# Two-layer decoder step: gate and value products on half the depth, seven for eight; down in parts of four; low parts of plain weights by adding transfers

## The chip, the cores and the metric

The kernel runs on one core of a Trainium2 chip. A core has five engines with instruction streams of their own: PE (TensorE, matrix products into PSUM), DVE (VectorE), ACT (ScalarE), POOL (GpSimd) and SP (SyncE, which here issues most transfers); 16 DMA engines move data between HBM and SBUF. The metric is device microseconds of one execution. It is taken over several runs, and the profile is of one further execution by the hardware profiler.

## The reference

One inference step of a decoder with two layers. Layer 0 mixes tokens by sliding-window attention, layer 1 by gated linear attention; each is followed by a feed-forward with a causal convolution of width 3 on its gate. There are 512 new rows of one sequence (the prompt) and 8 single rows (the samples). The model is 1024 wide, the feed-forward 2816. All is fp32. What the change touches is the feed-forward and the normalisation around it:

```python
def conv_ffn(x, buf, w_up, conv_w, conv_b, w_down):
    h = x @ w_up                                   # 1024 -> 2 * 2816
    a, u = h[..., :D_FF], h[..., D_FF:]            # gate, value
    ap = jnp.concatenate([buf.astype(a.dtype), a], axis=1)
    c = conv_b + sum(conv_w[j] * ap[:, j:j + T] for j in range(CONV_W))
    y = (jax.nn.gelu(c, approximate=False) * u) @ w_down
    return y, ap[:, T:]

# in each layer i, after the mixer:
xp = layer_norm(ALPHA * xp + mp, ln_mix_g[i], ln_mix_b[i])
fp, cp = conv_ffn(xp, buf0, ffn_w_up[i], ffn_conv_w[i], ffn_conv_b[i], ffn_w_down[i])
xp = layer_norm(ALPHA * xp + fp, ln_ffn_g[i], ln_ffn_b[i])
```

## The kernel before

Activations lie transposed: 128 features on the partitions, rows of tokens along the free axis. The 520 rows are two groups: a has 256 prompt rows, b has 256 prompt rows and the 8 samples (264). A matrix product of fp32 is made of three products in a shorter format (fp32r): each operand is split into a high part (a rounded copy, by ACT) and a low part (what is left, by DVE), and high x high, high x low and low x high are summed in PSUM.

All weights are loaded in *units* of 128 output features: one tile of 128 x 1024 (8 depth steps of 128). `plan` lists the units in order; `phases` marks where stretches of them begin. For layer 0: q, k, v and attention, then eight units of the output projection, then the feed-forward. For layer 1 the same with the gated linear attention. In the feed-forward, the 22 blocks of 128 gate and value features come in three parts, `FF_PARTS` = (0..6, 6..14, 14..22): for each block a unit for the gate and one for the value, and after each part eight down units of that part's depth, which add into x. The last part's down units also carry the normalisation (`ln_chunk`, `ln_end`).

`order` sets the order of the work: each unit is done for a and for b, a leading by four or five units. `load_unit` (L152) loads a unit: a transfer by SP into a `raw` tile (two buffers), then ACT makes `wh` (L167) and DVE `wl` (L170) in one of six weight slots; in the feed-forward there is a seventh slot, `wx`. `run` loads the next unit as soon as b's use of one is done. For a few units behind the start of a stretch the two conversions are issued later (`parts`, L181 and L183), so that they don't stand before the normalisation.

`product` (L186 to L205) issues the three matmuls of each depth step, with 256 or 264 columns. `product2` (L208 to L222), which group a uses in blocks 4 to 21 and in down parts 0 and 1, has high and low part of a's rows side by side and makes the two products with the high weights by one matmul of 512 columns; its two halves are added afterwards by DVE (L641, L663, L686). `ffn_gate` evacuates the gate from PSUM, applies the three taps and Gelu; `ffn_value` multiplies by the value and splits the result into `hh` and `hl` for down. PSUM has eight banks: four `accp` accumulators here, four for the rest (`mps`: two `sc`, one `tp`, one `pv`).

The scheduler that builds the engines' streams orders instructions by a planned timeline where no dependence or written order forbids it; on PE matmuls of neighbouring units can thus stand between one another.

After the normalisation that follows the mixer, POOL adds the bias to x (`ln_end`, L361) late, one chunk per unit, since only down needs it.

Of the kernel before, what the change touches and what calls it, by code (L numbers as in the profile page):

```python
# [11 lines left out]
F32 = mybir.dt.float32  # L12
F32R = mybir.dt.float32r
# [17 lines left out]
FF_PARTS = ((0, 6), (6, 14), (14, 22))  # L31
# [15 lines left out]
EXTRA = 1  # L47
XEND = 8
ACCS = 4

# [10 lines left out]

WIDE = 4
# [35 lines left out]
class Net:  # L98
    def __init__(self, tc, ctx, I, O):
# [9 lines left out]
        self.acc = pool("acc", ACCS, space=PSUM)  # L109
        self.mps = pool("mps", space=PSUM)  # L110
        self.dram = pool("dram", 2, space=DRAM)
# [38 lines left out]


    def load_unit(self, u, pieces=1, extra=False, late=False):  # L152
# [4 lines left out]
        r = self.raw.tile([P, KD * P], F32, name="raw")  # L157
        pool = self.wx if extra else self.wts
        h, l = (pool.tile([P, KD * P], F32R, name=name) for name in ("wh", "wl"))
        n = nt * P // pieces  # L160
        for c in (slice(i * n, (i + 1) * n) for i in range(pieces)):
# [8 lines left out]
            nc.vector.tensor_tensor(l[:, c], r[:, c], h[:, c].bitcast(F32), op=ALU.subtract)  # L170
        self.w[u] = (h, l)

# [35 lines left out]
    def product2(self, g, u, rs, rh, rl, wide):  # L208


        if rs is None or not wide:
            return self.product(g, u, rh, rl), None
        nc = self.nc
        h, l = self.w[u]
        nt = self.units[u][1]
        ps = self.acc.tile([P, 512], F32, name="accp")
        o = ps.rearrange("p (j t) -> p j t", t=2)
        for k in range(nt):
            ks = slice(k * P, (k + 1) * P)
            last = k == nt - 1  # L220
            both = lambda: nc.tensor.matmul(o, h[:, ks], in_turn(rs[:, k].rearrange("p t q j -> p t (q j)")), start=k == 0, stop=last)  # L221
            low = lambda: nc.tensor.matmul(o[:, :P], l[:, ks], in_turn(rh[:, k]), start=False, stop=False)  # L222
            for f in (low, both) if last else (both, low):
                f()
        return ps[:, :256], ps[:, 256:]
# [59 lines left out]
    def ln_end(self, g, i, last=False):  # L285
# [71 lines left out]
        if g.i == 0:  # L357
            self.norm = self.slot + HOLD, self.exp, v.ins, xl.ins, self.next_phase() + 1
        for m in range(KD):
            yield 1 if m else LATEB  # L360
            self.tc.keep_in_program_order(nc.gpsimd.tensor_scalar(x[:, m], x[:, m], 1.0, bi(m), op0=ALU.mult, op1=ALU.add))  # L361
# [243 lines left out]
    def ffn_open(self, layer):  # L605
        nc = self.nc
        if EXTRA:
            self.wx, self.wx_cm = self.open(f"wts{layer}", EXTRA)
# [564 lines left out]
```

## Time and profile before

| | |
|---|---|
| time, median of 2 runs | 1134.0 us (1132.05 to 1135.95) |
| span of the profiled execution | 1131.7 us |
| mean granted clock of PE | 0.991 |
| HBM read, written | 108.67 MB, 8.47 MB |
| share of the DMA engines, queue of SP | 32.8% |

The span runs from the first to the last instruction of the profiled execution; what lies around it belongs to the time of a run and not to the span. The page of the profile gives each engine's busy time, 40 slices of the span, the queues, the chain of work that ended last, and the costliest groups of instructions; other views give the same for a stretch or in order of time. In a row of a timeline stand start, length (both us), engine, line of the kernel, operation, what it writes and reads, shape and count; in brackets the idle time before it and what ended it. Matmuls are pipelined, so their records overlap, and the distance between two starts tells what one costs. The slices of the two engines with most to do, and what the transfers moved:

```profile
PE   8999999999999999999999999999999999999996
...
DVE  7897579655665566568867778779756665566565
...
GB/s 244 150 178 96 16 75 101 105 103 121 94 105 102 93 100 106 75 134 94 57 90 145 122 178 160 139 111 94 113 98 127 94 98 109 93 96 110 76 64 76
```

The feed-forward of layer 0 runs from about 167 to 530 us, that of layer 1 from about 765 to the end.

### The profile page before, as it was taken

How to read it: one execution, taken by the hardware profiler on the slowest of the kernel's cores; microseconds unless marked ns; L12 is line 12 of the kernel's file. 1: busy time of each engine (PE TensorE's matmuls, PEld its weight loads, DVE VectorE, ACT ScalarE, POOL GpSimd, SP SyncE). 2: the span in 40 equal slices, each digit the busy share in tenths (PEclk: the TensorE clock that was granted, in tenths of full speed). 3: DMA queues.
4: the chain of work that ended last, by engine and by line, in shares of the span. 5: the costliest groups of instructions: out<-in, count | busy, mean ns of one | idle time of the engine just before them, and what ended most of it. 6: DMA issues, size and time to landing. Idle time of an engine off the chain costs nothing.

```text
span 1131.7 us, 22912 instructions
## 1 busy us (share of the span) xinstructions
PE 1104.2 (98%) x8806; PEld 1055.1 (93%) x8806; DVE 777.2 (69%) x1626; ACT 565.7 (50%) x1251; POOL 319.3 (28%) x591
## 2 busy tenths in 40 slices
PE   8999999999999999999999999999999999999996
PEld 7997799999999999999899999899999999999995
DVE  7897579655665566568867778779756665566565
ACT  5677556534553245435455556456524553245433
POOL 4575574400110011255211100374400110001243
PEclk9999999999999999999899999999999999999998
DMA  7553023333233233242124354432333223223222
GB/s 244 150 178 96 16 75 101 105 103 121 94 105 102 93 100 106 75 134 94 57 90 145 122 178 160 139 111 94 113 98 127 94 98 109 93 96 110 76 64 76
DMA packets 53804, 122.81 MB, mean 109 GB/s; under 512 B 6808, under 2 KB 27328, under 8 KB 53696
## 3 DMA queue, kind: packets, MB, share of 16 engines
q1 hardware_dynamic: 51536, 119.47, 32.8%
q10 hardware_dynamic: 2160, 1.89, 0.5%
q8 instruction: 69, 1.13, 0.4%
q14 instruction: 39, 0.32, 0.1%
HBM read 108.67 MB, written 8.47 MB: 104 GB/s over the span
## 4 chain that ended last, share of the span: by engine, by line
PE 77%; DVE 10%; DMA 5%; ACT 3%; issue 2%; POOL 1%; SPq 0%; ACTq 0%; DVEq 0%; POOLq 0%
PE accp L198 16%; PE accp L200 16%; PE accp L202 16%; PE accp L221 15%; PE accp L222 8%; DMA vb<-dv 2%; DVE xs_a L355 1%; DVE wl L183 1%; DVE wl L170 1%; DMA raw<-in_w_up 1%; DMA qs<-hl 1%; DVE sgla L910 1%; DVE x_a L353 1%; PE pv L554 1%; ACT pr L523 1%
## 5 line engine op out<-in xcount | busy, mean ns | idle before, releaser
L170 DVE TENSOR_TENSOR wl<-raw,wh 128x1024 fp32r<-128x1024 f32 (+2 forms) x172 | 207.0, 1205 | 103.3 <-ACT wh L167 102.7
L198 PE MATMUL accp<-xh_b,wh 128*128 128x264 f32 x976 | 272.5, 279 | 1.8 <-ACT xh_b L354 1.7
L167 ACT ACTIVATE wh<-raw 128x1024 fp32r<-128x1024 f32 (+2 forms) x168 | 173.6, 1033 | 199.8 <-PE accp L200 187.3
L202 PE MATMUL accp<-xh_b,wl 128*128 128x264 f32 x976 | 270.8, 277 | 0.0
L200 PE MATMUL accp<-xl_b,wh 128*128 128x264 f32 x960 | 266.5, 278 | 0.0
L221 PE MATMUL accp<-xs_a,wh 128*128 128x512 f32 x576 | 196.3, 382 | 0.0
L198 PEld LDWEIGHTS accp<-xh_b,wh 128*128 128x128 f32 x976 | 184.8, 189 | 3.3 <-ACT xh_b L354 2.3
L202 PEld LDWEIGHTS accp<-xh_b,wl 128*128 128x128 f32 x976 | 184.5, 189 | 0.8 <-issue 0.6
L200 PEld LDWEIGHTS accp<-xl_b,wh 128*128 128x128 f32 x960 | 181.6, 189 | 2.5 <-issue 0.4
L222 PE MATMUL accp<-xs_a,wl 128*128 128x256 f32 x576 | 145.4, 273 | 0.0
L198 PE MATMUL accp<-hh_b,wh 128*128 128x264 f32 x480 | 134.2, 280 | 1.7 <-ACT hh_b L228 1.1
L200 PE MATMUL accp<-hl_b,wh 128*128 128x264 f32 x480 | 134.6, 280 | 0.3 <-DVE hl_b L594 0.2
L202 PE MATMUL accp<-hh_b,wl 128*128 128x264 f32 x480 | 133.6, 278 | 0.0
L221 PEld LDWEIGHTS accp<-xs_a,wh 128*128 128x128 f32 x576 | 109.1, 189 | 11.4
L222 PEld LDWEIGHTS accp<-xs_a,wl 128*128 128x128 f32 x576 | 110.2, 191 | 1.9
L198 PE MATMUL accp<-xs_a,wh 128*128 128x256 f32 x400 | 107.6, 284 | 1.4 <-ACT wh L167 0.6
L200 PE MATMUL accp<-xs_a,wh 128*128 128x256 f32 x384 | 103.0, 282 | 0.6 <-DVE xs_a L229 0.3
L198 PEld LDWEIGHTS accp<-hh_b,wh 128*128 128x128 f32 x480 | 91.6, 191 | 2.3 <-ACT hh_b L228 1.6
L200 PEld LDWEIGHTS accp<-hl_b,wh 128*128 128x128 f32 x480 | 91.5, 191 | 1.8 <-DVE hl_b L594 0.4
L202 PEld LDWEIGHTS accp<-hh_b,wl 128*128 128x128 f32 x480 | 91.5, 191 | 0.2
L232 POOL COPY hist<-aext 128x2 f32<-128x2 f32 x44 | 10.2, 231 | 283.7 <-DVE aext L641 277.2
L198 PEld LDWEIGHTS accp<-xs_a,wh 128*128 128x128 f32 x400 | 77.2, 194 | 2.8 <-ACT wh L167 1.0
(338 smaller groups left out, 2505.5 us busy)
## 6 DMA issues: line engine op xcount, KB each, us to landing
raw<-in_w_up SPq DMA_DIRECT2D x88, 512.0 KB, 3.4
raw<-in_w_down SPq DMA_DIRECT2D x32, 512.0 KB, 3.4
raw<-in_w_gla SPq DMA_DIRECT2D x24, 512.0 KB, 3.4
raw<-in_w_mix_o SPq DMA_DIRECT2D x16, 512.0 KB, 4.1
raw<-in_w_down SPq DMA_DIRECT2D x16, 384.0 KB, 3.0
qs<-hl SPq DMA_DIRECT2D x64, 64.0 KB, 2.2
sgla<-in_state_gla SPq DMA_DIRECT2D x16, 256.0 KB, 2.7
vb<-dv SPq DMA_DIRECT2D x16, 256.0 KB, 3.7
```

The source lines that it names most:

```text
L167: nc.scalar.activation(h[:, c], r[:, c], AF.Copy)
L170: nc.vector.tensor_tensor(l[:, c], r[:, c], h[:, c].bitcast(F32), op=ALU.subtract)
L183: self.nc.vector.tensor_tensor(l, r, h.bitcast(F32), op=ALU.subtract)
L198: nc.tensor.matmul(o, h[:, ks], xh, start=k == 0, stop=False)
L200: nc.tensor.matmul(o, h[:, ks], xl, start=False, stop=False)
L202: nc.tensor.matmul(o, l[:, ks], xh, start=False, stop=not tail and k == nt - 1)
L221: both = lambda: nc.tensor.matmul(o, h[:, ks], in_turn(rs[:, k].rearrange("p t q j -> p t (q j)")), start=k == 0, stop=last)
L222: low = lambda: nc.tensor.matmul(o[:, :P], l[:, ks], in_turn(rh[:, k]), start=False, stop=False)
L353: v = nc.vector.scalar_tensor_tensor(x[:, m], x[:, m], sc(m), rp, op0=ALU.mult, op1=ALU.mult)
L355: xl = nc.vector.scalar_tensor_tensor(g.xl[:, m], parted(x[:, m]), bi(m), g.xh[:, m].bitcast(F32), op0=ALU.add, op1=ALU.subtract)
L523: nc.scalar.activation(pr[:, b, 0:P + 1], sc[:, b, 0:P + 1], AF.Exp, bias=nm[:, b:b + 1], accum_out=den[:, b:b + 1])
L554: mm = nc.tensor.matmul(pv[64 * v:64 * v + 64, b * P:(b + 1) * P], self.vtok[:, kb, 64 * v:64 * v + 64], parts[v][w][:, b], start=i == 0, ...
```

## The change

It has four parts, all in the feed-forward of both layers.

**Seven products.** Blocks 0 to 3 stay as they were, but always by `product`. From block 4 on, gate and value of a block and groups a and b make one 2 x 2 product: outputs (gate, value) by (a, b), with the depth of 1024 cut into two halves. Instead of eight half-depth products, `ffn_pair` makes seven, of sums and differences of the halves (Winograd's form of Strassen's scheme): four use sums of weights (`s1` to `s4`), four use sums of rows (`t1` to `t4`), and the results are recombined by DVE. Each is 4 depth steps x 3 matmuls of 256 or 264 columns; 512-wide matmuls are gone. Gate and value of all 520 rows then lie in one tile, and taps, Gelu and the product with the value run over both groups at once. The results of six products go into two rotating PSUM tiles of two banks each (the four old accumulators are closed for this time and opened again behind block 21); the first goes into an `sc` bank.

**Sums.** `pair_tasks` prepares a block's weights in four tasks (two loads, sums by DVE, splits by ACT and DVE), of which three take one of the six weight slots each; `load_next` issues them as slots come free. `row_sums` and `row_sum1` make the sums of rows once a layer, during blocks 0 to 3: 16 operations of DVE and four splits by ACT and DVE, and four small splits for `t1`, which overwrites the first half of b's rows once block 3 is done. The bias shifts of x move into `row_sums`.

**Down in parts of four.** `FF_PARTS` is (0..4, 4..8, 8..12, 12..16, 16..22). The down units of a part of four (two output chunks in one unit, `ffn_down2`) stand between the blocks of the next part, one behind each of the first four. Their two chunks go to one double tile, and DVE adds both into x at once. The last part has eight units of depth 6 at the end, as before with the normalisation.

**Low parts by adding transfers.** For the plain weights of blocks 0 to 3, of the upper task and of `ffn_down2`, DVE no longer subtracts. ACT writes minus the high part, and a transfer issued by POOL adds the weights from HBM onto it. The seventh slot (`wx`) is gone, and `ffn_down2` has a raw tile of its own.

The diff, cut to its core:

```diff
-FF_PARTS = ((0, 6), (6, 14), (14, 22))
+FF_PARTS = ((0, 4), (4, 8), (8, 12), (12, 16), (16, 22))
+HSLOTS = 8
...
+PAIRED = 4
+WIDES = 2
...
-            nc.vector.tensor_tensor(l[:, c], r[:, c], h[:, c].bitcast(F32), op=ALU.subtract)
+            if self.units[u][2] in (self.ffn_gate, self.ffn_value, self.ffn_down2):
+                self.low_by_dma(l[:, c], h[:, c], src[:, c])
+            else:
+                nc.vector.tensor_tensor(l[:, c], r[:, c], h[:, c].bitcast(F32), op=ALU.subtract)
...
+    def low_by_dma(self, l, h, src):
+        self.nc.scalar.activation(l, h.bitcast(F32), AF.Copy, scale=-1.0)
+        self.nc.gpsimd.dma_start(out=l, in_=src, accum_op=ALU.add)
...
+        def upper():
+            r1, r0 = (self.raw.tile([P, KD * P], F32, name="raw") for _ in range(2))
+            nc.sync.dma_start(out=r1, in_=src1)
+            nc.sync.dma_start(out=r0, in_=src0)
+            h, l = slot()
+            nc.scalar.activation(h, r0, AF.Copy)
+            self.low_by_dma(l, h, src0)
+            keep(h, l, "a11", "a12")
...
+        def lower():
+            s = T["s"] = self.pp.tile([P, half], F32, name="sum3")
+            add(s, r1[:, lo], r0[:, lo])
+            add(r1[:, lo], r1[:, lo], r1[:, hi])
+            h, l = slot()
+            self.split(h, l, r1)
+            keep(h, l, "s1", "a22")
...
+        def sums():
+            add(r0[:, lo], r1[:, lo], r0[:, lo])
+            add(r0[:, hi], r0[:, lo], r0[:, hi])
+            h, l = slot()
+            self.split(h, l, r0)
+            keep(h, l, "s2", "s4")
...
+        def third():
+            h, l = (self.pp.tile([P, half], F32R, name=name, bufs=2) for name in ("wh3", "wl3"))
+            self.split(h, l, T["s"])
...
+    def ffn_pair(self, u, layer, j, q):
+        p1 = self.mtile("sc")
+        self.half_product(p1, W["a11"], part(a, lo), n)
+        v = self.ln.tile([P, NT - 256], F32, name="nv")[:, :n]
+        nc.scalar.copy(v, p1[:, :n])
+        p = self.wide()
+        self.half_product(p[:, 0], W["a12"], part(a, hi), n)
+        self.release()
+        self.half_product(p[:, 1], W["s2"], t2, m)
+        add(M[:, :, 2:2 + n], p[:, :, :n], both(v))
+        nc.scalar.copy(h[:, n:m], p[:, 1, n:m])
+        p = self.wide()
+        self.half_product(p[:, 0], W["s1"], t1, m)
+        self.half_product(p[:, 1], W["a22"], t4, n)
+        self.release()
+        add(C[:, :, :n], p[:, :, :n], both(h[:, :n]))
+        add(C[:, 0, n:], p[:, 0, n:m], h[:, n:m])
+        p = self.wide()
+        self.half_product(p[:, 0], W["s4"], part(b, hi), m)
+        self.release()
+        self.half_product(p[:, 1], W["s3"], t3, m)
+        self.half -= 1
+        self.load_next()
+        add(M[:, :, 2 + n:], p[:, :, :m], both(C[:, 0]))
+        add(h[:, :n], p[:, 1, :n], C[:, 1, :n])
...
+        nc.scalar.activation(c[:, :SEQ], g[:, 2:2 + SEQ], AF.Identity, scale=w(2), bias=cb)
+        nc.vector.scalar_tensor_tensor(c[:, :SEQ], g[:, 1:1 + SEQ], w(1), c[:, :SEQ], op0=ALU.mult, op1=ALU.add)
+        nc.vector.scalar_tensor_tensor(c[:, :SEQ], g[:, 0:SEQ], w(0), c[:, :SEQ], op0=ALU.mult, op1=ALU.add)
+        nc.vector.scalar_tensor_tensor(c[:, SEQ:], g[:, 2 + SEQ:], w(2), self.base[:, j], op0=ALU.mult, op1=ALU.add)
...
+        nc.scalar.activation(c, c, AF.Gelu)
+        nc.vector.scalar_tensor_tensor(h, c, -1.0, h, op0=ALU.mult, op1=ALU.mult)
+        self.split(a.hh[:, q], a.hl[:, q], parted(h[:, :n]))
+        self.split(b.hh[:, q], b.hl[:, q], parted(h[:, n:]))
...
+    def ffn_down2(self, u, layer, part, i):
+        for g in self.groups:
+            ps, n = self.wide(), g.n
+            for s in range(2):
...
+            x = g.x[:, 2 * i:2 * i + 2]
+            if part == 0:
+                nc.vector.scalar_tensor_tensor(x, x, ALPHA, ps[:, :, :n], op0=ALU.mult, op1=ALU.add)
+            else:
+                nc.vector.tensor_tensor(x, x, ps[:, :, :n], op=ALU.add)
+        self.release()
```

More of the change, by code (lines that the diff above doesn't have):

```diff
@@ L60 @@
 LOWS = 7
-WIDE = 4
 SPAUSE = 2
@@ L156, in load_unit @@
             return self.load_rank(u)
-        r = self.raw.tile([P, KD * P], F32, name="raw")
-        pool = self.wx if extra else self.wts
-        h, l = (pool.tile([P, KD * P], F32R, name=name) for name in ("wh", "wl"))
+        down = self.units[u][2] == self.ffn_down2
+        r = (self.pp if down else self.raw).tile([P, KD * P], F32, name="raw")
+        h, l = (self.wts.tile([P, KD * P], F32R, name=name) for name in ("wh", "wl"))
         n = nt * P // pieces
@@ L206, in product, with pair_tasks, keep @@
         return ps[:, :g.n]
[L208 to L218, printed above, removed]
-            ks = slice(k * P, (k + 1) * P)
[L220 to L225, printed above, removed]
+    def pair_tasks(self, u):
+        nc, half = self.nc, KD * P // 2
+        lo, hi = slice(0, half), slice(half, KD * P)
+        src0, src1 = self.units[u][0]
+        W, T = {}, {}
+        self.w[u] = W
+        add = lambda o, x, y: nc.vector.tensor_tensor(o, x, y, op=ALU.add)
+        slot = lambda: [self.wts.tile([P, KD * P], F32R, name=name) for name in ("wh", "wl")]
+        def keep(h, l, first, second):
+            W[first], W[second] = (h[:, lo], l[:, lo]), (h[:, hi], l[:, hi])
+        def upper():
[6 more added lines that the diff above has]
+            keep(h, l, "a11", "a12")
+            T.update(r0=r0, r1=r1)
+        def lower():
+            r0, r1 = T["r0"], T["r1"]
+            s = T["s"] = self.pp.tile([P, half], F32, name="sum3")
[5 more added lines that the diff above has]
+        def sums():
+            r0, r1 = T["r0"], T["r1"]
+            add(r0[:, lo], r1[:, lo], r0[:, lo])
[6 more added lines that the diff above has]
+            self.split(h, l, T["s"])
+            W["s3"] = h, l
+        return [("live", upper), ("live", lower), ("live", sums), ("half", third)]
@@ L618, in ffn_open @@
         b = self.par[:, C_CB + layer * NF:C_CB + (layer + 1) * NF].unsqueeze(2).broadcast_to([P, NF, NS])
-        t = p.tile([P, NF, NS], F32, name="baset")
+        self.pp, self.pp_cm = self.open(f"pair{layer}")
+        s = lambda i: [P, KD // 2, 2, (256 + NS * (i < 2)) // 2]
+        self.th, self.tl = ([self.pp.tile(s(i), F32R, name=f"{n}{i}") for i in range(3)] for n in ("th", "tl"))
+        self.cp, self.cp_cm = self.open(f"chain{layer}")
+        t = self.cp.tile([P, NF, NS], F32, name="baset")
         g = nc.gpsimd
@@ L685, in ffn_down @@
-        if lo is not None:
-            nc.vector.tensor_tensor(g.x[:, m], g.x[:, m], lo, op=ALU.add)
+        ps = self.product(g, u, g.hh, g.hl)
+        yield from self.ln_chunk(g, m, ps, True, last=layer == 1)
+        if m == KD - 1:
+            yield from self.ln_end(g, 2 * layer + 1, last=layer == 1)
     def gla_open(self):
@@ L1039, in run @@
                 pre()
[L1040 to L1053 removed]
+            self.slot += i + 1 if i == 2 else 1
+            if i == 2:
+                f(u, *a)
+            else:
+                self.resume(f(self.groups[i], u, *a))
+            if i == 1:
+                self.release()
             self.due()
```

244 lines of the change are left out of this document (172 added, 72 removed).

## The prediction

> **What bounds the kernel now.** I read the page first: the busy row, the slices, the chain's shares. Then the stretches of both feed-forwards, then the timeline of single engines inside one of them.
>
> ```profile
> span 1131.7 us, 22912 instructions
> PE 1104.2 (98%) x8806; PEld 1055.1 (93%) x8806; DVE 777.2 (69%) x1626; ACT 565.7 (50%) x1251; POOL 319.3 (28%) x591
> PEclk9999999999999999999899999999999999999998
> ```
>
> Of the stretches, then of the waits:
>
> ```profile
> 190.00:500.00 310.00, 310.00 (x2391) 299.29 (x2390) 190.39 (x354) 138.51 (x252) 48.33 (x138) 1.00 0.32 105
> 780.00:1090.00 310.00, 310.00 (x2385) 299.05 (x2386) 192.63 (x360) 140.73 (x258) 48.17 (x130) 1.00 0.31 100
> ```
>
> ```profile
> ACT wh L167 <- PE accp L200: 187.3, 123, 4.3
> ```
>
> The two stretch rows give length, then PE, weight load, DVE, ACT and POOL busy time, granted clock, DMA share and GB/s. Inside the feed-forwards PE has no idle microsecond in 310, at a clock of 1.00; DVE stands at 61 to 62%, DMA at 0.32. The wait row says that new weights wait for PE to give a slot back, so they are early. Only fewer PE microseconds shorten these 620 us. What one matmul costs is read from starts, since records overlap:
>
> ```profile
> 150.05 0.28 PE L198 MATMUL accp<-hs_a,wh 128*128 128x256 f32 x1
> ...
> 152.39 0.28 PE L198 MATMUL accp<-hh_b,wh 128*128 128x264 f32 x1
> ...
> 300.51 0.28 PE L198 MATMUL accp<-xh_b,wh 128*128 128x264 f32 x1
> ...
> 303.21 0.38 PE L221 MATMUL accp<-xs_a,wh 128*128 128x512 f32 x1
> 303.43 0.27 PE L222 MATMUL accp<-xs_a,wl 128*128 128x256 f32 x1
> ...
> 305.83 0.28 PE L198 MATMUL accp<-xh_b,wh 128*128 128x264 f32 x1
> ```
>
> 21 matmuls of 256 columns take 152.39 - 150.05 = 2.34 us, 0.1114 each; 24 of 264 take 303.21 - 300.51 = 2.70, 0.1125 each; a 512 takes 0.22, and a unit of eight 512 plus eight 256 takes 305.83 - 303.21 = 2.62. Time follows columns.
>
> **The products.** Before, a gate and value pair costs two units for group a and two for b: 2 x (2.62 + 2.70) = 10.64 us. After, it is seven products of 12 matmuls: three of 256 columns, four of 264: 36 x 0.1114 + 48 x 0.1125 = 9.41. The difference is 1.23, for blocks 4 to 21 of two layers, 36 pairs: 44.3 us. Giving up the 512-wide matmul in down parts 0 and 1 costs, for 14 depth steps x 8 units x 2 layers, 3 x 0.1114 - 2.62/8 = 0.007 us each: 224 x 0.007 = 1.5 back. The other regroupings of down keep their columns. Gross gain: 42.8.
>
> **VectorE, per pair.** Starts to the next start:
>
> ```profile
> 304.39 1.23 DVE L170 TENSOR_TENSOR wl<-raw,wh 128x1024 fp32r<-128x1024 f32 x1 [1.03 <-ACT wh L167]
> 305.53 0.22 DVE L648 SCALAR_TENSOR_TENSOR conv<-aext,par,base 128x8 f32<-128x8 f32 x1
> 305.67 0.48 DVE L643 SCALAR_TENSOR_TENSOR conv<-aext,par,conv 128x256 f32<-128x256 f32 x1
> 306.19 0.48 DVE L644 SCALAR_TENSOR_TENSOR conv<-aext,par,conv 128x256 f32<-128x256 f32 x1
> 306.59 0.42 DVE L663 TENSOR_TENSOR hprod<-hprod,accp 128x256 f32<-128x256 f32 x1
> ...
> 1111.83 1.88 DVE L335 TENSOR_TENSOR x_a<-x_a,pv 128x512 f32<-128x512 f32 x3
> 1113.62 0.43 DVE L282 TENSOR_TENSOR s_b<-s_b,x_b 128x264 f32<-128x264 f32 x1
> ```
>
> 1024 elements cost 1.14, 8 cost 0.14, 256 cost 0.40 (0.52 where the next waits for it), 512 cost 1.79/3 = 0.60. Weights of a pair: five half-width operations and two full ones, 5 x 0.60 + 2 x 1.14 = 5.3. Recombination, taps, product and low parts: six of about 0.60 with 0.12 twice for a dependent one, two of 0.14, three of 0.40, hence 5.3. Sum 10.6, beside 9.41 of PE. The 16 down units a layer, now without a subtraction, add 2 x 0.6 = 1.2 beside 48 x 0.112 = 5.37 of PE. A pair with its down unit: 11.8 of 14.78 us, 80%; the two last pairs of a layer have none and need 10.6 in 9.41, but part of their weights is prepared earlier in the freed 20%. I cost VectorE at nothing on average. The cover that matters is PSUM: two double tiles, so PE fills one for 24 x 0.112 = 2.7 us while the other is emptied. An emptying 0.60 behind a 1.14 subtraction fits; behind two it does not. Behind two of 1.14 and two of 0.60 it waits 2 x 1.14 + 3 x 0.60 - 2.7 = 1.4. Bounds: 0 and 1.4 once a pair; I take 0.1, because the usual 1.74 is under the cover: 36 x 0.1 = 3.6.
>
> **ScalarE and POOL.** A weight copy takes 0.96 from start to start:
>
> ```profile
> 303.30 1.06 ACT L167 ACTIVATE wh<-raw 128x1024 fp32r<-128x1024 f32 x1 [1.05 <-PE accp L200]
> 304.26 0.40 ACT L653 ACTIVATE conv<-conv 128x256 f32<-128x256 f32 x1
> ```
>
> The nearest row for a transfer's issue is in the chain of work:
>
> ```profile
> 84.28 0.62 SPq L478
> ```
>
> Six and a half of these (6.2) and some 3 us of chain per pair and down unit are 9.2 of 14.78: hidden. POOL gets two issues of perhaps 0.62 in that time. Behind them stand copies of convolution state that nobody awaits before the layer's end.
>
> **The adding transfers.** No row shows one. A copy of 512 KiB lands 3.4 us after issue; at 105 GB/s for a share of 0.32 it fills all engines for 524 KB / 328 GB/s = 1.6 us.
>
> ```profile
> raw<-in_w_up SPq DMA_DIRECT2D x88, 512.0 KB, 3.4
> ...
> vb<-dv SPq DMA_DIRECT2D x16, 256.0 KB, 3.7
> ```
>
> An adding one can hardly beat a copy (1.6); its top is the slowest row per byte, 3.7 for 256 KB, thus 7.4. I take 3.2, two copies, being nearest to the copy row and because what is added onto must be read too. The Trainium skill, "Collectives: The Full Stack", section "The bandwidth ceiling: the fold count and why AG ≠ RS ≠ AR", says that an adding transfer is slower for its two source reads, not for the add; by that it is also 3.2, and no run here shows it yet. Per pair and down unit there are three copies and two adding ones: 3 x 1.6 + 2 x 3.2 = 11.2 of 14.78, under the bound. With six slots a pair's first is the one freed after the sixth product of the pair two before; then 1.35 + 5.37 of that period and a whole one of 14.78 follow, 21.5 us in which 1.92 of ScalarE and 3.4 to 7.4 of landing are hidden. It isn't at a layer's start: without the extra slot, units 6 and 7 get theirs only when b's units 0 and 1 are done, and then need 2 x 0.96 plus the landing. The covers are b's next units (2.70 each) and the unit's own high parts (16 x 0.11 = 1.8): waits of 0 to 1.92 + 7.4 - 4.5 = 4.8, four times: 0 to 19. PE's order does interleave units where one is late:
>
> ```profile
> 185.74 0.28 PE L202 MATMUL accp<-xh_b,wl 128*128 128x264 f32 x1
> 185.85 0.27 PE L198 MATMUL accp<-xs_a,wh 128*128 128x256 f32 x1
> ...
> 186.75 0.38 PE L198 MATMUL accp<-xh_b,wh 128*128 128x264 f32 x1
> ```
>
> So I take 0.75 each, 3.0.
>
> **The first four blocks.** The row sums for the seven products are new VectorE work here: 4 x 0.34 twice, five of 1024 (5.7), six tiny ones, four low parts: about 10.5 us. In its eight units VectorE is already full:
>
> ```profile
> 166.70:209.40 42.70, 41.68 (x346) 40.42 (x346) 37.17 (x71) 26.25 (x53) 16.64 (x30) 1.00 0.37 120
> ```
>
> ```profile
> 166.70:209.40 42.70, 5.61 (x5) 1.00 0.37 120
> ```
>
> (The first row is of all engines, DVE the fourth number of time; the second of the five subtractions at L170 alone.) 37.2 - 5.6 + 10.5 + 7.6 for the first pairs' weights is 49.7 in 42.7 us: up to 7 late per layer, 0 if the second pair's 2.3 and the idle of the next stretch absorb it. I take 2.5 a layer, 5.0: the 7.0 less the deferrable 2.3, half of that met by idle time. At POOL the shifts of x only change place.
>
> **The ends.** Block 21 feeds a's first down unit directly, where before four b units lay between. From conv to low part the old 256-wide chain runs from 304.83 to 308.4:
>
> ```profile
> 304.83 0.57 ACT L642 ACTIVATE conv<-accp,par 128x256 f32<-128x256 f32 x1
> ...
> 307.98 0.43 DVE L229 TENSOR_TENSOR hs_a<-hprod,hs_a 128x256 fp32r<-128x256 f32 x1 [0.52 <-ACT hs_a L228]
> ```
>
> That is 3.6; twice as wide and with two adds ahead some 5.8. Fifteen matmuls (1.7 us) of each open unit need only older blocks, and four banks allow four: wait 0 to 4.1; I take 1.5 a layer, 3.0, for two and a half open units. Then the normalisation of a, which in layer 0 PE needs next:
>
> ```profile
> 510.10 0.41 DVE L250 TENSOR_TENSOR x_a<-x_a,accp 128x256 f32<-128x256 f32 x1
> ...
> 519.79 0.90 DVE L355 SCALAR_TENSOR_TENSOR xs_a<-x_a,par,xs_a 128x256 fp32r<-128x256 f32 x1
> ```
>
> 9.7 us, covered by four b units of 2.70 = 10.8. They shrink to 18 x 0.1125 = 2.03 each, 8.1: 0 to 2.7 uncovered, I take 2.7, once, since 8.1 is below 9.7 already and POOL's part gets denser. The last normalisation ends the kernel either way: 0.
>
> **Sum.** 42.8 - 3.6 - 3.0 - 5.0 - 3.0 - 2.7 = 25.5. The profiled span is 1131.7; the median of the runs shown is 1134.0, 2.3 above, which stays. 1134.0 - 25.5 = 1108.5, told as 1108.
>
> **Rivals.**
> - VectorE empties PSUM too late: its 80% and the bare pairs' 10.6 in 9.41 speak for it, the order planned ahead against it. At 1.0 per pair 36 replaces 3.6: 1108 + 32 = 1140, no change to be told. It costs 0.9 per pair to lose the whole gain.
> - Slower: the adding transfers saturate the 16 engines. Three copies and two adding ones pass 14.78 once one takes 5.0; from 5.4 on (32 periods x 0.8 = 26) the kernel is slower than before. At 6.4, four copies: 17.6 per period, 32 x 2.8 = 90, 1198. Against it: 5.4 is over three copies' time.
> - The change saves no PE time, because narrow matmuls are bound by their weight loads (PEld at 93%). Seven products need 84 loads where 80 were: 4 more in 80, so it would end near 1134 plus its waits, 1150. The rows above, 0.22 against 0.11 for twice the columns, reject it.
>
> The Trainium skill, "TensorE: Matmul & The Clock Gate", section "Back-to-back issue gap", gives a sustained 81 ns at 128 columns and 131 at 512; as an estimate about 98 at 256, by which a pair would gain 0.1 us and the kernel nothing. This case's trace disagrees: 0.22 at 512, 0.111 at 256.
>
> **How the numbers follow.** The forecast, with its waits anywhere inside their bounds but not all at the top, gives 1091 (1134 - 42.8, no wait) to 1111: chance 0.52. VectorE late, or several of the start's and ends' waits near their tops: 1112 to 1155: 0.32. Adding transfers: 0.14. Weight loads: 0.02. About 2% (22.7 us) is what a measurement of this kernel can tell from no change. Faster by over that is below 1111: 0.52; within: 0.32 + 0.02 = 0.34; slower: 0.14. The range 1091 to 1146 leaves out the transfers' case and the upper end of the second.
>
> **What will show it.** PE starts in a half product stay 0.111 to 0.1125 apart, and a pair with its down unit takes 14.8 us; PE idle before the second half of a pair with VectorE as its releaser means the first rival; adding transfers that share the engines above 0.9 mean the second. Idle PE at units 6 and 7, before block 4 and after block 21 shows the three waits. Wrong I would be by a period above 15.8 us, or by waits at block 4 over 7 us.

## The result, and the profile after

The changed kernel takes 1183.2 us (median of two runs, 1181.9 to 1184.5) where the kernel before takes 1134.0: a ratio of 1.044, with a 95% interval of 1.039 to 1.049. It is slower by 49 us; 1108 had been forecast. The profiled execution has a span of 1182.7 us, 0.5 below the median. Of the four runs of e1 below, the profiled one was in a slow state (1270.8 us), so its time and ratio in the table are those of the other three.

From the page of the kernel after: span, busy times, the slices of TensorE and of its clock, the queue of the adding transfers (packets, MB, share of 16 engines' span) and two kinds of transfer (number, KB each, median us from issue to landing).

```profile
span 1182.7 us, 23889 instructions
PE 1095.6 (93%) x9174; PEld 1055.4 (89%) x9174; DVE 896.1 (76%) x1778; ACT 657.5 (56%) x1307; POOL 356.2 (30%) x565
PE   9999996899999999999999999997799999999995
PEclk9999998999999999999899999997989999999998
q0 software_dynamic: 10656, 38.80, 19.6%
raw<-in_w_up SPq DMA_DIRECT2D x88, 512.0 KB, 4.2
wl<-in_w_up POOLq DMA_DIRECT2D x42, 512.0 KB, 6.4
```

TensorE was 98% busy before and is 93% now; the gaps sit at the start of each feed-forward (slices 7, 8, 28 and 29 of 40), and the granted clock falls there too (7, 28 and 30). There are 74 adding transfers, 42 of gate and value weights and 32 of down weights; one takes 0.196 x 1182.7 / 74 = 3.13 us of the 16 engines, and lands 6.4 us after its issue.

A long stretch inside the blocks by pairs in layer 0, in the columns of the stretch rows of before (TensorE's time in layer 1 is the same within 0.2 us):

```profile
250.00:500.00 250.00, 240.45 (x2113) 237.91 (x2112) 190.21 (x318) 140.93 (x205) 34.59 (x61) 1.00 0.68 162
```

TensorE now lacks 10 us in 250, where nothing was lacking; the transfers take 0.68, not all. What TensorE waited for, over the whole span (total, times, longest):

```profile
PE sc L284 <- DMA wl<-in_w_up: 15.6, 15, 1.7
PE accp L216 <- ACT wh L177: 9.5, 4, 4.2
PE widep L282 <- DVE hprod L775: 9.2, 2, 5.1
PE accp L223 <- DMA wl<-in_w_up: 7.0, 2, 4.0
...
PE accp L216 <- ACT xh_b L413: 4.1, 4, 1.5
PE accp L223 <- DVE xl_b L414: 2.9, 6, 1.1
PE widep L860 <- DVE merged L799: 2.8, 4, 1.2
```

The first row is the steady part. The next three are the starts: per layer one long wait for unit 6's high part, one for the PSUM banks that block 3's last product with the value still holds, one for unit 6's low part. The rows with `xh_b` and `xl_b` are starts too: TensorE waits for the normalisation of b. The last row is the down unit's second group, whose double tile is not empty yet. In the kernel before, the longest total of the starts was this:

```profile
PE accp L198 <- ACT xh_b L354: 1.7, 2, 0.9
```

**Where the 49 us come from.** TensorE's timeline gives the ends of the stages:

```profile
165.46 0.27 PE L216 MATMUL accp<-xs_a,wh 128*128 128x256 f32 x1
...
235.53 0.38 PE L282 MATMUL widep<-xs_a,wh 128*128 128x256 f32 x1 [4.12 <-DVE hprod L775]
...
506.87 0.35 PE L216 MATMUL accp<-hs_a,wh 128*128 128x256 f32 x1 [2.09 <-DVE merged L799]
...
784.96 0.27 PE L216 MATMUL accp<-xs_a,wh 128*128 128x256 f32 x1
...
857.69 0.55 PE L282 MATMUL widep<-xs_a,wh 128*128 128x256 f32 x1 [5.05 <-DVE hprod L775]
...
1131.05 0.35 PE L216 MATMUL accp<-hs_a,wh 128*128 128x256 f32 x1 [2.08 <-DVE merged L799]
```

| stage | measured, layer 0 and 1 | TensorE's work | too much, both layers | forecast |
|---|---|---|---|---|
| start: eight units and the first `sc` product | 70.1 and 72.7 | 8 x 5.37 + 1.35 = 44.3 | 54.2 | 8.0 |
| blocks 4 to 21 with 16 down units | 271.3 and 273.4 | 18 x 9.41 + 16 x 5.37 - 1.35 = 253.9 | 36.9 | 3.6 + 3.0 |

The work of a unit, 24 x (0.1114 + 0.1125) = 5.37, and of a pair, 9.41, is that of the prediction. So the waits are 46 and 30 us above forecast, together 76; the result is 75 above it. By the distances between TensorE's starts, the 54 of the starts are about 27 in the six long waits with the restart behind each, 12 in waits for the normalisation and 12 in matmuls at half the clock; 18 of the 37 of the second stage are waits for the adding transfer.

### The profile page after: what moved, and what is told of

The parts are those of the page before. It is cut to its first block, busy times and chain, and to the rows that moved or that the text cites. A ratio compares the mean times of both kernels' runs of the same rounds, so it can differ in the third digit from the quotient of the medians.

```text
span 1182.7 us, 23889 instructions
## 1 busy us (share of the span) xinstructions
PE 1095.6 (93%) x9174; PEld 1055.4 (89%) x9174; DVE 896.1 (76%) x1778; ACT 657.5 (56%) x1307; POOL 356.2 (30%) x565
## 3 DMA queue, kind: packets, MB, share of 16 engines
q0 software_dynamic: 10656, 38.80, 19.6%
## 5 line engine op out<-in xcount | busy, mean ns | idle before, releaser
L282 PE MATMUL widep<-th,wh 128*128 128x264 f32 (+1 forms) x432 | 120.0, 278 | 0.0
L283 PE MATMUL widep<-tl,wh 128*128 128x264 f32 (+1 forms) x432 | 119.9, 278 | 0.0
L284 PE MATMUL widep<-th,wl 128*128 128x264 f32 (+1 forms) x432 | 119.8, 277 | 0.0
L216 PE MATMUL accp<-xh_b,wh 128*128 128x264 f32 x400 | 115.6, 289 | 4.1 <-ACT xh_b L413 4.1
L220 PE MATMUL accp<-xh_b,wl 128*128 128x264 f32 x400 | 113.5, 284 | 0.0
L218 PE MATMUL accp<-xl_b,wh 128*128 128x264 f32 x384 | 108.5, 283 | 0.0
L288 DVE TENSOR_TENSOR wl<-raw,wh 128x1024 fp32r<-128x1024 f32 x72 | 86.7, 1220 | 10.4 <-ACT wh L287 10.1
L216 PEld LDWEIGHTS accp<-xh_b,wh 128*128 128x128 f32 x400 | 77.5, 194 | 6.4 <-ACT xh_b L413 4.9
L282 PEld LDWEIGHTS widep<-th,wh 128*128 128x128 f32 x432 | 83.0, 192 | 0.0
L283 PEld LDWEIGHTS widep<-tl,wh 128*128 128x128 f32 x432 | 83.0, 192 | 0.0
L284 PEld LDWEIGHTS widep<-th,wl 128*128 128x128 f32 x432 | 82.9, 192 | 0.0
L284 PE MATMUL widep<-xh_b,wl 128*128 128x264 f32 x288 | 79.6, 277 | 0.0
```

The lines of the kernel that those rows point to most:

```text
L216: nc.tensor.matmul(o, h[:, ks], xh, start=k == 0, stop=False)
L218: nc.tensor.matmul(o, h[:, ks], xl, start=False, stop=False)
L220: nc.tensor.matmul(o, l[:, ks], xh, start=False, stop=not tail and k == nt - 1)
L282: self.nc.tensor.matmul(o, h[:, ks], rh, start=k == 0, stop=False)
L283: self.nc.tensor.matmul(o, h[:, ks], rl, start=False, stop=False)
L284: self.nc.tensor.matmul(o, l[:, ks], rh, start=False, stop=k == KD // 2 - 1)
```

## The experiments

The ratio is that to runs of the kernel before made beside each; 0.01 is 11.3 us. The kernel after stands at 1.0436 (1.0385 to 1.0488).

| run | what differs from the kernel after | us | ratio, 95% interval |
|---|---|---|---|
| e1 | value weights of a pair in the down units' raw tile | 1253.7 | 1.1043 (1.1008 to 1.1077) |
| e2 | upper low part by DVE | 1173.6 | 1.0339 (1.0323 to 1.0356) |
| e3 | low parts of blocks 0 to 3 by DVE | 1182.1 | 1.0421 (1.0404 to 1.0438) |
| e4, e7 | seventh slot | 1170.6, 1169.7 | 1.0317 (1.0294 to 1.0339), 1.0314 (1.0281 to 1.0348) |
| e5 | value weights in a raw tile of their own | 1190.2 | 1.0490 (1.0458 to 1.0522) |
| e6 | no row sums | 1178.5 | 1.0373 (1.0312 to 1.0434) |
| e8 | seventh slot, upper low by DVE, double tiles flipped | 1156.4 | 1.0195 (1.0163 to 1.0227) |
| e9 | first product in written order | 1174.5 | 1.0354 (1.0324 to 1.0385) |
| e10 | e9, seventh slot, flip | 1155.5 | 1.0198 (1.0183 to 1.0213) |
| e11 | e10, upper low by DVE | 1157.5 | 1.0216 (1.0191 to 1.0242) |
| e12 | kernel before, without its seventh slot | 1150.5 | 1.0150 (1.0127 to 1.0172) |
| e13, e14 | e10, block 3's chain first; pair 5's weights held too | 1153.3, 1153.3 | 1.0151 (1.0119 to 1.0183), 1.0156 (1.0131 to 1.0182) |
| e15 | e14 without row sums | 1152.8 | 1.0153 (1.0121 to 1.0184) |
| e16 | shifts of x on ScalarE | 1177.8 | 1.0384 (1.0354 to 1.0413) |
| e17 | e14, shifts on ScalarE | 1148.7 | 1.0116 (1.0092 to 1.0140) |
| e18 | e17, pair 5's weights behind block 3's chain | 1154.4 | 1.0169 (1.0147 to 1.0191) |

**The steady part: raw tiles, or the transfer?** My first theory was a loop through the two raw tiles, which both loads of a pair occupy until the last of its splits.

```diff
 # e1
-            r1, r0 = (self.raw.tile([P, KD * P], F32, name="raw") for _ in range(2))
-            nc.sync.dma_start(out=r1, in_=src1)
-            nc.sync.dma_start(out=r0, in_=src0)
+            r0, r1 = (p.tile([P, KD * P], F32, name="raw") for p in (self.raw, self.pp))
+            nc.sync.dma_start(out=r0, in_=src0)
+            nc.sync.dma_start(out=r1, in_=src1)
 # e2
-            self.low_by_dma(l, h, src0)
+            nc.vector.tensor_tensor(l, r0, h.bitcast(F32), op=ALU.subtract)
```

> The upper task's second load (value weights) goes to the raw tile of the down units instead of the general pair of raw tiles, so that gate weights alternate between two tiles; nothing else moves and no memory is added. Theory A (the two raw tiles close a loop over two periods: Gelu, splits, release of raw, load, copy, negation, adding transfer, first product): the gate weights no longer wait for the previous block's splits, the lost PE time of 15.7 us in 250 to 500 us falls below 6, and the time to 1150 to 1165. Rival B (the adding transfer itself is late because the DMA engines are crowded): share and landing stay, lost time stays near 15, time 1178 to 1188. The starts of the feed-forwards keep their loss (about 26 us each) under both.

> Only the upper task's low part is made by DVE's subtraction (1.14 us per pair) again, blocks 0 to 3 and down keep adding transfers. Theory A: the loop is shorter by negation, issue and landing (1.06 + 0.86 + about 5.5) less 1.14, so lost PE time in 250 to 500 falls below 6 and the time to 1150 to 1165. Rival B (crowded engines): the same, as 36 of 74 adding transfers are gone. Rival C (DVE at 76% is what is late): lost time stays or grows, 1180 to 1200. With the run before it: if both fall, the raw tiles; if this alone falls, the transfers.

e1 was a miss: 70 us slower still. The down unit now shares its raw tile with the value weights, and SP works through its queue in order, so the next gate weights stand behind a down load that cannot start. Waits of SP's queue in e1 from 300 to 500 us:

```profile
SPq L172 <- DVE wl L288: 76.9, 11, 7.0
```

It says that sharing a tile costs much, not that a further one would help. e2 took the waits for the upper low part away and won about 10 us; it didn't reach the 1150 to 1165 expected. It can't tell the loop from the transfer. So the third tile was tried by itself:

```diff
 # e5
-            r1, r0 = (self.raw.tile([P, KD * P], F32, name="raw") for _ in range(2))
+            r1 = self.pp.tile([P, KD * P], F32, name="raw1")
+            r0 = self.raw.tile([P, KD * P], F32, name="raw")
...
-            h, l = (self.pp.tile([P, half], F32R, name=name, bufs=2) for name in ("wh3", "wl3"))
+            h, l = (self.pp.tile([P, half], F32R, name=name) for name in ("wh3", "wl3"))
...
-                if self.half == 2:
+                if self.half == 1:
```

> The value weights of a pair get a raw tile of their own (the space comes from the third split, which is single instead of double); adding transfers stay as they are. Theory A (raw tiles close the loop, the transfer's 5 to 8 us only lengthen it): first products wait for their low part no longer, as in the run with the upper low part by DVE, period 15.2 to 15.5 us instead of 15.9, time 1165 to 1176. Rival B (the transfer behind ScalarE's order is late however early the weights are loaded): PE's waits for the adding transfer of in_w_up stay above 10 us a layer, time 1180 to 1190.

TensorE in e5 (its L285 is L284 of the kernel after):

```profile
PE sc L285 <- DMA wl<-in_w_up: 21.0, 19, 1.7
```

The wait grew from 15.6 to 21.0: the third tile did not help. (It doesn't rule raw tiles out by itself. The value weights are loaded first and wait for their one tile, so the gate weights behind them in SP's queue come no earlier, and the third split has one buffer instead of two; a third tile with the loads in the other order wasn't tried.) What is the cause stands in the timeline of the kernel after. Here is one pair's gate weights, from load to use: SP, ScalarE, POOL, then TensorE:

```profile
381.15 0.33 SPq L243 DMA_DIRECT2D raw<-in_w_up  x1
...
385.95 1.06 ACT L245 ACTIVATE wh<-raw 128x1024 fp32r<-128x1024 f32 x1 [1.20 <-PE widep L283]
387.05 1.07 ACT L188 ACTIVATE wl<-wh 128x1024 fp32r<-128x1024 f32 x1
...
388.41 0.86 POOL L189 DMA_DIRECT2D wl<-in_w_up  x1 [2.50 <-ACT wl L188]
...
395.81 0.38 PE L284 MATMUL sc<-xs_a,wl 128*128 128x256 f32 x1 [0.91 <-DMA wl<-in_w_up]
...
408.03 0.27 PE L282 MATMUL widep<-xs_a,wh 128*128 128x256 f32 x1
```

The matmul at 395.81 belongs to the first product of a pair whose other products begin at 408.03. Its written place is just before them; it stands some 11 us ahead of that, between the products of the pair before, and TensorE waits there for the adding transfer, with the other products behind it. The next run only puts this product back:

```diff
 # e9, for the first product of a pair only
-            self.nc.tensor.matmul(o, h[:, ks], rh, start=k == 0, stop=False)
+            first = self.nc.tensor.matmul(o, h[:, ks], rh, start=k == 0, stop=False)
+            if late and k == 0:
+                self.tc.keep_in_program_order(first)
```

> The kernel after, but each pair's first product (the one in the sc bank) keeps its written place on PE, behind the down unit of the pair before; the planner had moved it 12 to 15 us ahead, between the products of the pair before. Theory D (the adding transfer lands early enough for the written order, 379.22 us for a pair that begins near 391, and PE waits only because the first product was moved ahead of it): PE's waits for in_w_up's adding transfer fall from 35 us to under 5 in all, the first pair's sc matmuls no longer stand before block 3, lost time in 250 to 500 us from 15.7 to under 8: 1160 to 1172. Rival A' (the loop of splits, load, copy, negation and transfer is itself longer than a period, wherever the product stands): the wait moves to the new place and the time stays at 1178 to 1188. Rival (the moved product filled PE while the double tiles are emptied): the low part's waits go, but waits for DVE or ACT at the double tiles grow by as much, 1178 or more.

In e9, TensorE and POOL around the same pair, and the longest waits of TensorE between 250 and 1110 us:

```profile
387.64 0.86 POOL L189 DMA_DIRECT2D wl<-in_w_up  x1 [0.41 <-ACT wl L188]
...
390.10 0.27 PE L282 MATMUL sc<-xs_a,wh 128*128 128x256 f32 x1
...
405.34 0.27 PE L282 MATMUL sc<-xs_a,wh 128*128 128x256 f32 x1
```

```profile
PE widep L862 <- DVE merged L801: 9.1, 20, 1.6
```

The transfer issued at 387.64 has until 405.34, 17.7 us; the waits for it are gone from the list. The time fell by about 9 us, as in e2 (e9's interval touches that of the kernel after). e11, below, adds the DVE subtraction to the written order: 1157.5 against 1155.5, no gain. So theory D holds: in the written order the transfer is hidden. The last rival holds in part: the 20 waits for DVE at the down unit's second group, whose double tile DVE has not emptied, are 9.1 us where the kernel after had 2.8, so the moved product had filled some of that time. From 390.10 to 405.34 a pair with its down unit takes 15.24 us; 14.78 was forecast.

**The start: slot, low parts, row sums.**

```diff
 # e3
-            if self.units[u][2] in (self.ffn_gate, self.ffn_value, self.ffn_down2):
+            if self.units[u][2] in (self.ffn_down2,):
 # e4, e7: unit 6 goes where the third split goes later; low part by DVE (late=True)
+        self.s3 = [self.pp.tile([P, KD * P], F32R, name=name) for name in ("wh3", "wl3")]
+        self.extra = self.nu - 1
+        self.todo.clear()
+        self.load_unit(self.extra, late=True, slot=self.s3)
...
-        r = wide(self.raw.tile([P, KD * P], F32, name="raw"))
+        r = wide(self.pp.tile([P, KD * P], F32, name="raw"))
 # e7 only: no third split before unit 6 is used up
+        self.half = 2
...
+            if i == 1 and u == self.extra:
+                self.half = 0
```

> Only the three units a layer of blocks 0 to 3 that had an adding transfer get their low part by DVE. Theory A (at the start PE waits for units 6 and 7: slot, copy, negation, POOL behind its shifts, transfer): the gaps of 4.2 and 3.2 us on the low part of unit 6 go, with the clock they cost, 6 to 10 us a layer, time 1165 to 1172; the gap of 4.6 on its high part stays. Rival (DVE is full there, so the subtraction is just as late): within 4 us of 1183, and the wait at block 4 grows by 2 to 3 us a layer.

> The seventh unit of each feed-forward is loaded ahead again, into the place that the third split uses later, with its low part by DVE, and the row sums use the down units' raw tile. Theory A (the lost slot is the cause of the start's first two gaps): 4.6 + 4.2 us and 4.6 + 3.2 go together with the slow clock behind them, 10 to 16 us a layer: 1152 to 1163. Rival (normalisation of b and DVE are late anyway): the gap moves to the next unit and less than 8 us in all are won, 1175 or more.

> As the fourth run (seventh unit ahead in the place of the third split, its low part by DVE, row sums in the down units' raw tile), but the third split waits until that unit is used up. Theory (the lost slot makes the first two gaps of the start): 4.6 + 4.2 and 4.6 + 3.2 us go with their slow clock, something of it comes back at the first pair, whose weights are prepared later: 1165 to 1173. Rival (all comes back at the first pair): 1178 to 1186.

Of the eight units of blocks 0 to 3 only three a layer have an adding transfer (42 = 36 pairs + 6); the low parts of the others, whose conversions are issued late, are still made by DVE. In e4 the third split may overwrite unit 6 before group b has used it, so block 3's gate is partly made with other weights; its time is that of e7. e3 is the same as the kernel after, within the interval: the gap of 4.0 us on the low part went, and the one at the first double tile grew from 4.1 to 5.9. TensorE in e3, then in e7, from 160 to 250 us:

```profile
PE widep L282 <- DVE hprod L775: 5.9, 1, 5.9
```

```profile
PE widep L283 <- DVE hprod L781: 6.0, 1, 6.0
```

With the slot back (e7) both of unit 6's waits go and 13.5 us are won; part moves to the double tile. The same slot taken from the kernel before costs more:

```diff
 # e12, in the kernel before
-EXTRA = 1
+EXTRA = 0
```

> The kernel before, only without its seventh weight slot (six slots throughout the feed-forward). If the slot is worth at the start what the runs on the kernel after say (13 us for two layers), and nothing in the steady part: 1140 to 1150. If the steady part needs it as well: above 1155. If the start's loss comes from other parts of the change: 1133 to 1138.

e12 is 17 us slower (1.3 to 1.7%), though its longest wait at the start is 2.2 us; the upper end of what was expected for the start alone. The steady part doesn't need the slot: from the first to the last 512-wide matmul of layer 0 both kernels take 263.1 us. Then the row sums were left out (e6 and e15 don't compute `t1` to `t4`):

```diff
 # e6
-        self.t1 = [...]
...
-            self.split(self.th[q][:, :, :, n:], self.tl[q][:, :, :, n:], even(ts[:, q]))
...
-            self.row_sum1()
+        for t in (*self.th, *self.tl):
+            nc.gpsimd.memset(t.bitcast(F32), 0.0)
```

> The row sums and their splits are left out (the tiles t1 to t4 hold zeros or the old rows), the shifts of x stay. Theory (DVE, full in blocks 0 to 3, is late with the last block's product with the value, which holds the PSUM banks of the first pair): the waits of 4.3 and 5.2 us at the first double tile fall below 1.5 each, time 1168 to 1176. Rival (the order on ScalarE and DVE, the next pairs' weights standing ahead of the last block's chain, makes the wait): it stays above 3 us a layer, time 1178 to 1184.

TensorE in e6, from 160 to 250 us:

```profile
PE widep L282 <- DVE hprod L762: 2.3, 1, 2.3
PE accp L216 <- ACT wh L177: 2.2, 1, 2.2
```

The wait at the double tile halves, 4.1 to 2.3: neither theory has it whole. The wait for unit 6's high part halves too, 4.1 to 2.2. In time e6's interval (1.031 to 1.043) reaches the kernel after's; the profiled run took 1169.2, 9 us below e6's median.

**Do the causes add up?**

```diff
 # e8, e10 (the flip)
             self.open_wide()
+            self.wide()
```

e8 is e7 with e2's edit and the flip; e10 is e7 with e9's edit and the flip; e11 is e10 with e2's edit.

> Three things together: the seventh slot as in the run before, the upper task's low part by DVE, and the two double tiles of PSUM taken in the other order, so that the first pair's first double product does not need the banks of the last value product of block 3. If they add up: 1183 less 10 (upper) less 12 (slot) less 4 to 10 (both layers' wait at the first pair): 1150 to 1158. If the wait at the first pair only moves to the second double tile, 2.7 us later: 1157 to 1164.

> The first product in its written place, the seventh slot ahead, the double tiles in the other order; the upper low part stays with adding transfers. If the causes add up (order 13, slot 13, flip 4): 1150 to 1156. If the order only helps where DVE also made the low part: 1165 to 1172.

> As the run before, with the upper low part by DVE as well. Theory D: with the first product in its place the transfer is hidden and DVE's subtraction buys nothing more, it only adds 1.14 us of DVE a pair: equal to the run before or up to 8 us slower. Rival A': 8 to 12 us faster than the run before.

They do, within the intervals: order (e9) 9 and slot (e7) 14 make 23, and e10 is 27 us below the kernel after by the ratios. The other 4 might be the flip's, which wasn't run alone, but the intervals are as wide. The flip alone doesn't remove the wait for block 3's last product at the double tiles: it is 0.6 us in e8 and 12.2 in e10, over both layers, and the two take the same time.

**What is left of the start.** The last five runs went after the first pair's wait.

```diff
 # e13
-            self.row_sum1()
+            with self.tc.issue_after(self.gelu), self.tc.issue_after(self.last):
+                self.row_sum1()
 # e14, besides: the slot freed by unit 5 isn't filled before block 3 is written
+            elif i == 1 and u + 1 == self.extra:
+                self.live -= 1
 # e16, e17: in row_sums
-            self.shift(b, i, half + k)
+            self.shift_act(b, i, half + k)   # nc.scalar.activation(x, x, AF.Identity, bias=bi)
...
 # e18, besides
+                with self.tc.issue_after(self.gelu), self.tc.issue_after(self.last):
+                    self.release()
```

> As the run with order, slot and flip (1155), but the four splits for t1 stand behind block 3's Gelu on ScalarE and behind its last product with the value on DVE. Theory (order: that last product, at 228.59 us, holds the first double tile, and these splits and the next pair's weights stand before it): the waits of 7.0 and 5.5 us shrink by 2 to 3 each, time 1148 to 1153. Rival (amount: DVE is full): the wait only changes its name, 1153 to 1158.

> As the run before it, and pair 5's weights are not taken up before block 3's chain is written. Theory (order): the wait at the first pair is below 1.5 us a layer, 1142 to 1149, unless pair 5 then waits for its weights (a wait at its first low part, up to 5 us). Rival (amount): 1152 to 1158.

> As the run before it, with the row sums and their splits left out (tiles t1 to t4 hold zeros or the old rows). Theory (order): within 5 us of the run before it. Rival (amount of DVE work in blocks 0 to 3): 10 to 20 us faster than it, with the waits for accp and xl_b in the first 20 us of each feed-forward gone.

e13 and e14 are 2 us below e10 by the medians and 5 by the ratios, with intervals that touch, and e15 is no faster: with the row sums gone another wait takes their place in layer 0, 4.2 us for the adding transfer of unit 7. So the amount of the row sums is not what holds the time, and moving the splits for t1 is not enough. The third suspect was POOL. In the kernel after, the negation of unit 6 and then POOL's stream:

```profile
197.92 1.05 ACT L188 ACTIVATE wl<-wh 128x1024 fp32r<-128x1024 f32 x1
...
198.26 3.09 POOL L428 TENSOR_SCALAR x_b<-x_b,par 128x264 f32<-128x264 f32 x4
...
202.80 0.89 POOL L189 DMA_DIRECT2D wl<-in_w_up  x1
```

The low part is ready to be added to at 199.0 and its transfer is issued at 202.8, behind shifts of x and copies; TensorE waited 4.0 us for it. Before, the shifts went one per unit; now 16 stand nearly in a row.

> The kernel after, with the 16 bias shifts of the layer's start on ScalarE (about 0.45 us each) instead of POOL (about 0.9). Theory (POOL's queue delays unit 6's adding transfer by 3.8 us): the waits of 4.2 and 3.2 us on its low part fall below 1, with the slow clock behind them 8 to 12 us in both layers: 1171 to 1176. Rival (ScalarE's queue gets as full as POOL's was, or the transfer's own 6 us are the wait): 1179 to 1188.

> The kernel with first product in order, seventh slot, chain first and held weights (1153), with the shifts on ScalarE. Theory (POOL's queue delays the copies for the taps, on which DVE waits 2.25 us at 201 us, and PE 3.2 us for hprod): the gaps of 3.4 us at 202 and 809 us go: 1143 to 1149. Rival (DVE itself is late): 1151 to 1157.

> As the run before it, with pair 5's weights behind block 3's chain on ScalarE and DVE as well. Theory (the next pair's weights stand before block 3's last product with the value): the wait of 4.4 us at the first double tile shrinks to 1.5 to 2.5, 4 to 7 us less than the run before it. Rival (pair 5's weights are then late in their turn): the same time or up to 4 us more.

TensorE in e16, 160 to 250 us:

```profile
PE accp L220 <- DMA wl<-in_w_up: 0.5, 1, 0.5
```

Unit 6's wait for its low part (L223) is gone, and 0.5 is left at the next unit: POOL's queue had made it. The time fell by 5 to 6 us, less than expected and with intervals that overlap; the wait for the high part stayed at 3.7. On top of e14 the same edit gave 4.6 us, again with intervals that overlap, e17 being the best version at 1148.7, still 1.2% above the kernel before.

What is left in e17 is 9.3 us at the first double tiles of both layers. e18 takes this wait away: with the next pair's weights behind the chain, block 3's last product with the value, which holds the banks, runs 4.3 us earlier. DVE in e17, then in e18:

```profile
221.01 0.42 DVE L787 TENSOR_TENSOR hprod<-conv,accp 128x264 f32<-128x264 f32 x1
```

```profile
216.70 0.43 DVE L787 TENSOR_TENSOR hprod<-conv,accp 128x264 f32<-128x264 f32 x1
...
236.82 0.69 DVE L234 TENSOR_TENSOR sum<-raw 128x512 f32<-128x512 f32 x1 [9.85 <-DMA raw<-in_w_up]
```

So the order on ScalarE and DVE made the wait. But e18 is 6 us slower, as its rival said: a later pair's sums then stand for 9.85 us before a load, with the emptying of a double tile behind them, and TensorE waits 4.9 us for that and 3.1 for a copy that ScalarE makes late.

## Why the prediction was wrong

Two stages miss by most: the starts, told at 8.0 and measured at 54.2, and the blocks by pairs, told at 6.6 and measured at 36.9.

**The products: right.** The time of a matmul stayed what it was: in the kernel after ten of 256 columns lie between 376.72 and 377.83, 0.111 each. 84 matmuls, 36 of them with 256 columns and 48 with 264, make the 9.41 us of a pair.

```profile
376.72 0.28 PE L283 MATMUL widep<-xs_a,wh 128*128 128x256 f32 x1
...
377.83 0.28 PE L284 MATMUL widep<-xs_a,wl 128*128 128x256 f32 x1
```

**Adding transfers hidden in the steady part: the step that failed there.** The term "3.2 us of the engines each" was right (3.13), and the lead was nearly right for the written order: 21.5 us less the 1.92 of ScalarE's are 19.6 from the issue, and e9 has 17.7. But the lead was counted to where the pair stands in the code, though the prediction itself had shown a row where TensorE's order interleaves units. The planner moved the first product some 11 us forward, and TensorE reached its low part some 6.5 us after the issue, a microsecond before it had landed (the row at 395.81). TensorE waited 15.6 us in all, where nothing had been told; putting the order right won 9 of time.

**VectorE at the double tiles.** 0.1 us a pair was taken, bounds 0 to 1.4. With the order mended, this is layer 0 of e9 from the first double product to the first down matmul behind block 21:

```profile
238.45 0.42 PE L282 MATMUL widep<-xs_a,wh 128*128 128x256 f32 x1 [4.28 <-DVE hprod L777]
...
504.01 0.35 PE L216 MATMUL accp<-hs_a,wh 128*128 128x256 f32 x1 [1.67 <-DVE merged L801]
```

These 265.6 us are 11.7 above 253.9. Of that 1.7 is the wait at the end, and as much is lost at half the clock behind the wait at the start. Some 8 are left, 0.45 a pair, nearly all at ten waits for the down unit's second group with the restart behind each; layer 1 is alike. The first rival's mechanism was right, at half its price; its place is the down unit's second group and not the pair's second half. A mis-sized term: 3.6 told, about 16 measured (TensorE's list itself names 9.1).

**Late transfers at units 6 and 7.** Taken at 0.75 x 4 with bounds of 0 to 4.8 each. Unit 6 alone waited 4.1 and 4.2 us for its high part, and 4.0 and 3.0 for its low part. Three steps failed. The covers were wrong: a's unit 6 stands right behind b's unit 0 in TensorE's order, so nothing covers the copy of its high part, which can't start before b's unit 0 is done (at 193.3). ScalarE wasn't free: it made the copy only at 196.3, behind the taps' operations and a split of the row sums that waited for DVE.

```profile
195.29 1.14 ACT L287 ACTIVATE th<-raw 128x1024 fp32r<-128x1024 f32 x1 [0.71 <-DVE raw L447]
196.32 1.05 ACT L177 ACTIVATE wh<-raw 128x1024 fp32r<-128x1024 f32 x1
```

Without row sums (e6) 2.2 of this wait are left. And "at POOL the shifts of x only change place" passed over POOL's queue: the transfer stood behind them for 3.8 us. The slot is worth 13.5 us here (e7) and 17 in the kernel before (e12), where no adding transfer is.

**VectorE in blocks 0 to 3.** 5.0 told; the waits at the first double tile were 9.2 together. The direction was right; that the late piece would be the one that holds the PSUM banks was not seen. Nor was the normalisation of b, into which DVE's row sums now fall: TensorE waits 4.1 and 2.9 us for its parts, where it waited 1.7 before.

**The slow clock** was in no term. It is in the last section.

**The ends: nearly right.** 1.5 a layer behind block 21, measured 2.09 and 2.08. For the normalisation of a in layer 0, 2.7 was told; TensorE's waits for it, from 500 us on, are 2.5 and 0.9 now, beside 2.6 for another reason before, so about 1.

**The slower rival** (the transfers fill the 16 engines) named the right outcome for a wrong reason: share 0.68 where it asked for above 0.9, and 3.13 us where it needed 5.4. In e9 the share is 0.71 and the waits for these transfers are gone. The transfer's latency and its place in two streams, POOL's and TensorE's, decided, not its bandwidth. The rival on weight loads is out: 0.111 at 256 columns.

## What to carry to other kernels

A transfer's lead is to be counted to the place where its user stands in the engine's stream, not in the code; where a planner may move the user, pin it or look at the order. An operation handed to a queue (POOL's issue of a transfer, SP's next load) is late by all that stands in front of it there, so a moved block of small work can cost more than the work. A buffer that covers a restart is worth more than its share of steady time: each uncovered restart here cost a long wait, and then the clock.

## What the runs showed of the hardware

Behind its long waits TensorE ran at half its clock for some time. Kernel after, around the wait for unit 6's high part (stretch rows; the clock is the last but two):

```profile
192.00:197.50 5.50, 1.41 (x4) 0.73 (x4) 5.16 (x12) 3.36 (x6) 5.50 (x8) 0.50 0.01 1
197.50:202.00 4.50, 4.50 (x23) 4.50 (x24) 2.80 (x6) 2.97 (x6) 4.44 (x9) 0.55 0.38 117
```

Behind a wait of 4.1 us the clock is 0.50 to 0.55 for 4.5 us, in which 23 matmuls are done that need 2.6 us at 0.1125: about 2 us lost besides the wait; from 202 to 204 us it is 1.00 again. With three such waits a layer that is some 12 us in all, as an estimate. Waits of 1 to 2 us in the steady stretch left the clock at 1.00. In e12 a shorter wait, with little work around it, was enough:

```profile
193.00:196.00 3.00, 0.74 (x4) 0.43 (x4) 2.23 (x7) 2.39 (x6) 0.41 (x3) 1.00 0.00 0
196.00:202.00 6.00, 6.00 (x41) 6.00 (x41) 1.36 (x2) 0.61 (x3) 1.05 (x1) 0.72 0.24 87
```

The Trainium skill, "TensorE: Matmul & The Clock Gate", Part 1 ("The HAM clock gate"), says that after an idle window of about 3.4 us the clock is halved, and full again after a busy window of the same length. The 0.50 and the recovery agree. e12's wait of 2.2 us is shorter than that window, and the clock fell to 0.72 behind it all the same: there the measurement decides, and no run here shows how a window with a few matmuls in it is judged.

The other surprise is how far an adding transfer's two prices lie apart: 3.13 us of engine time as forecast, 6.4 from issue to landing where a plain load of the same size takes 4.2, and 0.86 us of POOL for the issue. The Trainium skill, "DMA: Bandwidth & Descriptors", section "SWDGE vs HWDGE vs iDMA", says that accumulating transfers can only be issued by GpSimd; no run here tried another queue.
